# Two 256-column instructions in place of one of 512, for the products of the two gate groups

## The chip, the cores and the metric

The kernel runs on one core of one Trainium2 chip. The metric is device time in microseconds (us) of one execution; smaller is better. The engines that matter here are TensorE (PE in the profile; its weight loads are listed apart as PEld), VectorE (DVE), ScalarE (ACT) and SyncE (SP, which issues the large loads from HBM).

## The reference

One layer of a hybrid encoder, for 256 tokens of width 4096, in float32. Cut to what matters:

```python
xn = rms_norm(x, norm_g)
h = jnp.einsum('bsd,de->bse', xn, w_in)          # w_in: 4096 x 14336
c_val, c_glu, c_gate, q, k, v, a_gate = jnp.split(h, split_pts, axis=-1)   # 2048 each
conv_out = conformer_conv(c_val, c_glu, ...) * jax.nn.silu(c_gate)
attn_out = longnet_mixture(rms_norm(q), rms_norm(k), v, rel_bias) * jax.nn.silu(a_gate)
x = x + jnp.einsum('bse,ed->bsd', concat([conv_out, attn_out]), w_out)     # 4096 x 4096
```

The change concerns the columns `c_gate` of the first product, 2048 of its 14336.

## The kernel before

**The products.** Each float32 operand is split into a high part of reduced width (type `fp32r`) and a low part (the rest, `fp32r` too). A product of two operands is then three matmuls: high by high, low by high, and high by low. The activations are the stationary operand, `xh` and `xl` (for the last product `mh` and `ml`), 128 rows of the contraction by 128 tokens; the weights stream past as the moving operand, `wh` and `wl`, 512 columns an instruction.

**Groups and steps.** The columns of both weight matrices are cut into 18 groups of 1024 columns, in this order: four groups `conv`, four pairs of `agv` and `qk` (attention gate and value, then query and key), two groups `gate`, and four groups `out`. Each group runs over 32 steps `k` of 128 contraction rows. Each step has two halves `e` of 512 columns, and each half has two blocks `s` of 128 tokens; a pair of half and block has an accumulator `acc` of 128x512 float32 in PSUM, a whole PSUM bank. So a step issues 2 halves x 2 blocks x 3 = 12 large matmuls, and the program has 18 x 32 x 12 = 6912 of them, 768 in the two gate groups.

**The order.** It is written by hand: `products(n, e, part)` issues part 0 (lines 668 and 669, with `wh`) or part 1 (line 671, with `wl`) of step n and half e. The loop at the end of the kernel issues half 0 of step n, half 1 of step n-1, and between them `split_w(n + 3)`, in which ScalarE makes `wh` (line 223) and VectorE makes `wl` (line 224) of a later step, and SyncE starts the load of a pair of steps behind it (line 202). `pump()` then adds units of background work: the convolution, norms, transposes, and the attention heads, whose two small float32 products stand on lines 521 (`psc`, scores) and 560 (`po`, values). After the last step of a half `evacuate` reads its two accumulators; for the gate groups this is a Silu on ScalarE (line 626).

Each matmul in the trace has a weight load (LDWEIGHTS, in the row of PEld) of its own, with the same line number.

Of the kernel before, what the change touches and what calls it, by code (L numbers as in the profile page):

```python
# [21 lines left out]
KT = D // P  # L22
# [18 lines left out]


def _bias_index():
    """[33, 512]: one-hot relative-position bucket of delta = column - 255, and in the
    last row the log of how many dilation patterns hold that delta."""
    out = np.zeros((RB + 1, NDEL), np.float32)
    half, exact, dmax = RB // 2, RB // 4, 1024
    for m in range(NDEL):
        d = m - (S - 1)
        n = abs(d)  # L50
        if n < exact:
            b = n
        else:
            b = exact + int(
                np.float32(np.log(np.float32(n) / np.float32(exact)))
                / np.float32(math.log(dmax / exact))
                * np.float32(half - exact)
            )
            b = min(b, half - 1)
        b += half if d > 0 else 0  # L60
        out[b, m] = 1.0
        c = int(n <= 64) + int(n % 4 == 0 and n <= 256) + int(n % 16 == 0 and n <= 1024)
        out[RB, m] = math.log(c) if c else NEG
    return out


class Lane:
    """Background work: generators that yield the weight of a unit on VectorE and ScalarE."""

    def __init__(self, width):  # L70
        self.gens = deque()
# [3 lines left out]
        self.gens.append(gen)  # L75

    def step(self, left):
        """One unit of each of the first generators, while both engines have room left."""
        spent = 0
        for gen in list(self.gens)[: self.width]:  # L80
            if min(left) <= 0:
                break
            try:
                cost = next(gen) or 0
            except StopIteration:
                self.gens.remove(gen)
                continue
            cost = cost if isinstance(cost, tuple) else (cost, 0)
            for i in range(2):
                left[i] -= cost[i]  # L90
            spent += sum(cost)
        return spent
# [3 lines left out]
def layer_kernel(  # L96
# [16 lines left out]
    nc = tc.nc  # L113
# [7 lines left out]
    def t4(name):  # L121
        return sb.tile([P, 4, 256], F32, tag="c4", bufs=15, name=name)
# [7 lines left out]
    def side(name):  # L130
        return ps.tile([P, 512], F32, tag="side", bufs=4, name=name)
# [8 lines left out]
        nc.tensor.transpose(dst, src, ident[:n, :n])  # L140

    def rsqrt(src, shape, mul, eps, name):
        """1 / sqrt(src * mul + eps), one Newton step after the table's square root."""
        n = int(np.prod(shape[1:]))
        tag = "rs_small" if n <= 32 else "rs_big"
        v = sb.tile(shape, F32, tag=tag, bufs=6, name=name + "v")
        r = sb.tile(shape, F32, tag=tag, bufs=6, name=name + "r")
        t = sb.tile(shape, F32, tag=tag, bufs=6, name=name + "t")
        cost = 60 + n
        nc.vector.tensor_scalar(v, src, mul, eps, op0=ALU.mult, op1=ALU.add)  # L150
        yield cost
        nc.scalar.activation(r, v, AF.Sqrt)
        yield
        nc.vector.reciprocal(r, r)
        nc.vector.tensor_mul(t, r, r)
        yield 3 * cost
        nc.vector.tensor_mul(t, t, v)
        nc.vector.tensor_scalar(t, t, -0.5, 1.5, op0=ALU.mult, op1=ALU.add)
        nc.vector.tensor_mul(r, r, t)
        yield 3 * cost  # L160
        return r
# [13 lines left out]
    groups = []  # L175
# [159 lines left out]
    conv_ready = {}  # L335

    def backwards(ap):
        """The last axis read from its end."""
        *lead, (step, n) = ap.ap
        return bass.AP(  # L340
            tensor=ap.tensor, offset=ap.offset + (n - 1) * step, ap=[*lead, [-step, n]]
        )

    def turn(tile_, name, flip=False):
        """[128 tokens, 2, 512 columns] to [128 columns, 4, 256 tokens], in its place: VectorE
        turns the blocks of 32, ScalarE puts them where they belong. With flip, the tokens of
        each half come in reversed order."""
        tmp = t4(name)
        src = tile_.rearrange("p a b -> p (a b)")
        flat = tmp.rearrange("p a b -> p (a b)")  # L350
        for s in range(2):
            nc.vector.transpose(flat[:, 512 * s : 512 * s + 512], src[:, 512 * s : 512 * s + 512])  # L352
            yield 620
        blocks = flat.rearrange("p (s t b x) -> p s t b x", s=2, t=4, b=4)
        dst = src.rearrange("p (t s a x) -> p s t a x", t=4, s=2, a=4)
        for b in range(4):
            for a in range(4):
                v = blocks[32 * a : 32 * a + 32, :, :, b, :]
                to = 3 - a if flip else a
                nc.scalar.copy(  # L360
                    dst[32 * b : 32 * b + 32, :, :, to, :], backwards(v) if flip else v
                )
                if a % 2 == 1:
                    yield 0, 620
# [34 lines left out]
        return bass.AP(tensor=ap.tensor, offset=ap.offset, ap=[ap.ap[0], [0, 4], [1, S]])  # L399

    def channel_mean(srcs, name):
        """Mean over all channels of four [128, 4, 256] tiles, on every partition, in PSUM."""
        tot = sb.tile([P, S], F32, tag="rs_big", bufs=6, name=name + "tot")
        for i, make in enumerate(srcs):
            v = make()
            if i:
                part = sb.tile([P, S], F32, tag="rs_big", bufs=6, name=f"{name}p{i}")
            else:
                part = tot
            nc.vector.reduce_sum(part, v.rearrange("p t s -> p s t"), axis=AX.X)  # L410
            yield 1135
            if i:
                nc.vector.tensor_add(tot, tot, part)
                yield 335
        yield
        yield
        pm = side(name + "pm")
        nc.tensor.matmul(pm[:, :S], ones, tot, start=True, stop=True)
        yield
        return pm  # L420
# [84 lines left out]
    def head_gen(hg, hh):  # L505
# [43 lines left out]
        for b in range(4):  # L549
            for a in range(4):  # L550
                nc.scalar.copy(  # L551
                    dst[32 * b : 32 * b + 32, :, :, 3 - a, :],
                    backwards(blocks[32 * a : 32 * a + 32, :, :, b, :]),
                )
            yield 0, 800
# [33 lines left out]
    left = [0, 0]  # L589

    def pump():
        """Background work for one step of the products: what the engines have room for."""
        for i, quota in enumerate((DVE_STEP, ACT_STEP)):
            left[i] = min(left[i] + quota, quota)
        mix_lane.step(left)
        fg.step(left)
        for _ in range(8):
            if not conv_lane.step(left):
                break
# [47 lines left out]
    accs = {}  # L647

    def products(n, e, part):
        """Products of step n into half e; part 0: with the weights' high parts, 1: with the low."""  # L650
        g, k = divmod(n, KT)
        if k == 0 and part == 0:
            accs[(g, e)] = [
                ps.tile([P, 512], F32, tag="acc", bufs=4, name=f"acc{g}_{e}_{s}") for s in range(2)
            ]
        if g < n_in:
            h, l = xh[k], xl[k]
        else:
            while k not in mh:
                pump()  # L660
            h, l = mh[k], ml[k]
        at = 512 if groups[g][3 + e] > groups[g][4 - e] else 0
        w = w_split[n][part][:, at : at + 512]
        for s in range(2):
            a = accs[(g, e)][s]
            hs, ls = h[:, P * s : P * s + P], l[:, P * s : P * s + P]
            if part == 0:
                nc.tensor.matmul(a, hs, w, start=k == 0, stop=False)  # L668
                nc.tensor.matmul(a, ls, w, start=False, stop=False)  # L669
            else:  # L670
                nc.tensor.matmul(a, hs, w, start=False, stop=k == KT - 1)  # L671
        if part == 1:
            if k == KT - 1:
                evacuate(g, e, accs.pop((g, e)))
            if e == 1:
                del w_split[n]

    load_x(0, 0, P)
    first = load_pair(0, pieces=2)
# [25 lines left out]
    for n in range(NG * KT):  # L705
        g, k = divmod(n, KT)
# [4 lines left out]
        if groups[g][0] == "out" and k in (8, 12):  # L711
            e = (k - 8) // 4
            c = groups[g][3 + e]
            t = t4(f"xr{g}_{e}").rearrange("p a b -> p (a b)").rearrange("p (s c) -> p s c", s=2)
            nc.sync.dma_start(t, xs[:, :, c : c + 512])
            xr_tiles[(g, e)] = t
        products(n, 0, 0)
        if n == 0:
            split_w(1)
# [26 lines left out]
        elif n == 29:  # L746
            list(rstd_steps)
        pump()


_BIAS_INDEX = _bias_index()
_INS = [
    "x", "norm_g", "w_in", "q_norm_g", "k_norm_g", "rel_bias", "conv_w", "conv_b",
# [30 lines left out]
```

## Time and profile before

| | |
|---|---|
| time, median of 2 runs | 1621.97 us (1621.79 to 1622.15) |
| span of the profiled execution, first to last instruction | 1620.2 us |
| PE busy (matmuls, ends modelled) | 1614.1 us, 100% of the span, 7146 instructions |
| PEld busy (weight loads, beside PE) | 1333.3 us, 82%, 7146 |
| DVE busy | 1074.4 us, 66%, 1440 |
| ACT busy | 926.8 us, 57%, 1415 |
| HBM traffic over the span | 196 GB/s |

The 7146 matmuls are the 6912 large ones and 234 small ones. The span stands 1.8 us below the median of the timed runs; that is what lies around the instructions. A matmul's recorded duration overlaps the next one's, so the spacing of their starts, or the chain of waits, tells what one costs; the duration does not.

### The profile page before, as it was taken

The page shows a single profiled execution, that of the slowest core. Times are in us where ns is not written, and L with a number is a line of the kernel's source. Part 1 is how long each engine was busy: PE and PEld are TensorE (multiplying, and loading weights), DVE is VectorE, ACT ScalarE, POOL GpSimd, SP SyncE. Part 2 cuts the span into 40 slices and gives each one's busy share as a digit, 9 for nine tenths or more (in the row PEclk, how much of TensorE's full clock was granted, in tenths as well). Part 3 has the DMA queues.
Part 4 walks back from the last instruction along what each step waited for, and adds up shares of the span by engine and source line. Part 5 has one row for each costly group of instructions (what it writes and reads, how often), then busy time and mean ns, then how long its engine had stood idle before and what let it go on. Part 6 is the DMA issues. An engine that isn't in the chain of part 4 may idle for free.

```text
span 1620.2 us, 19251 instructions
## 1 busy us (share of the span) xinstructions
PE 1614.1 (100%) x7146; PEld 1333.3 (82%) x7146; DVE 1074.4 (66%) x1440; ACT 926.8 (57%) x1415; POOL 2.7 (0%) x10
## 2 busy tenths in 40 slices
PE   9999999999999999999999999999999999999998
PEld 7788888888888888888888888888888888888887
DVE  5567888888888888768765555656466565454543
ACT  6564454545363556774778756774667973333332
POOL 0000000000000000000000000000000000000000
PEclk9999999999999999999999999999999999999999
DMA  8566565656656565656655666556555567666663
GB/s 311 192 188 202 184 204 184 199 191 193 196 189 201 186 203 194 192 160 204 191 187 188 187 202 192 191 166 200 195 197 179 195 214 225 217 218 223 213 228 104
DMA packets 140767, 319.39 MB, mean 197 GB/s; under 512 B 8639, under 2 KB 12049, under 8 KB 140672
## 3 DMA queue, kind: packets, MB, share of 16 engines
q1 hardware_dynamic: 140624, 318.13, 60.5%
q8 instruction: 56, 0.92, 0.2%
q14 instruction: 39, 0.32, 0.1%
q10 hardware_dynamic: 48, 0.02, 0.0%
HBM read 313.89 MB, written 4.23 MB: 196 GB/s over the span
## 4 chain that ended last, share of the span: by engine, by line
PE 99%; ACT 1%; issue 0%; DVE 0%; DVEq 0%
PE acc L668 32%; PE acc L669 32%; PE acc L671 32%; PE psc L521 1%; PE po L560 1%; PE xT L140 0%; ACT wh L223 0%; ACT cT L446 0%; PE spin L695 0%; ACT qk L360 0%; PE pw L140 0%; DVE wl L224 0%; PE pb L327 0%; DVE qk L501 0%; DVE xr L609 0%
## 5 line engine op out<-in xcount | busy, mean ns | idle before, releaser
L224 DVE TENSOR_TENSOR wl<-raw,wh 128x1024 fp32r<-128x1024 f32 x576 | 704.8, 1224 | 509.2 <-ACT wh L223 508.8
L223 ACT CAST wh<-raw 128x1024 fp32r<-128x1024 f32 x576 | 605.8, 1052 | 618.1 <-PE acc L669 412.6
L668 PE MATMUL acc<-wh,xh 128*128 128x512 f32 x1792 | 704.0, 393 | 0.0
L669 PE MATMUL acc<-wh,xl 128*128 128x512 f32 x1792 | 698.0, 390 | 0.0
L671 PE MATMUL acc<-wl,xh 128*128 128x512 f32 x1792 | 490.2, 391 | 0.0
L668 PEld LDWEIGHTS acc<-wh,xh 128*128 128x128 f32 x1792 | 336.5, 188 | 71.3 <-ACT xh L253 0.9
L669 PEld LDWEIGHTS acc<-wh,xl 128*128 128x128 f32 x1792 | 336.5, 188 | 70.2
L671 PEld LDWEIGHTS acc<-wl,xh 128*128 128x128 f32 x1792 | 334.3, 188 | 68.7 <-DVE wl L224 0.4
L392 DVE SCALAR_TENSOR_TENSOR cT<-conv,wT,cT 128x241 f32<-128x241 f32 (+14 forms) x480 | 201.6, 470 | 0.0
L668 PE MATMUL acc<-wh,mh 128*128 128x512 f32 x512 | 199.2, 389 | 0.0
L669 PE MATMUL acc<-wh,ml 128*128 128x512 f32 x512 | 199.2, 389 | 0.0
L671 PE MATMUL acc<-wl,mh 128*128 128x512 f32 x512 | 138.1, 389 | 0.0
L669 PEld LDWEIGHTS acc<-wh,ml 128*128 128x128 f32 x512 | 96.1, 188 | 20.0
L671 PEld LDWEIGHTS acc<-wl,mh 128*128 128x128 f32 x512 | 96.1, 188 | 19.9
L668 PEld LDWEIGHTS acc<-wh,mh 128*128 128x128 f32 x512 | 96.1, 188 | 19.9
L551 ACT COPY pr<-turn_p 32x128 f32<-32x128 f32 x256 | 75.9, 297 | 5.5 <-DVE turn_p L545 2.1
L253 ACT ACTIVATE xh<-xT,g_cols 128x256 fp32r<-128x256 f32 x32 | 15.2, 474 | 34.0 <-PE xT L140 33.9
L360 ACT COPY qk<-turn_q 32x256 f32<-32x256 f32 x64 | 25.9, 404 | 1.2
L360 ACT COPY qk<-turn_k 32x256 f32<-32x256 f32 x64 | 25.8, 404 | 1.2 <-DVE turn_k L352 0.2
L360 ACT COPY conv<-turn_a 32x256 f32<-32x256 f32 x64 | 25.8, 404 | 1.0
L360 ACT COPY agv<-turn_ag 32x256 f32<-32x256 f32 x64 | 25.8, 404 | 1.0
L360 ACT COPY gate<-turn_g 32x256 f32<-32x256 f32 x64 | 25.8, 404 | 1.0
(138 smaller groups left out, 428.0 us busy)
## 6 DMA issues: line engine op xcount, KB each, us to landing
raw<-in_w_in_dram SPq DMA_DIRECT2D x384, 512.0 KB, 4.9
raw<-in_w_out_dram SPq DMA_DIRECT2D x64, 1024.0 KB, 5.4
raw<-in_w_in_dram SPq DMA_DIRECT2D x32, 1024.0 KB, 5.0
xr<-in_x_dram SPq DMA_DIRECT2D x8, 512.0 KB, 6.0
out_dram<-xr SPq DMA_DIRECT2D x16, 256.0 KB, 4.7
x<-in_x_dram SPq DMA_DIRECT2D x6, 512.0 KB, 8.6
T<-bias_dram SPq DMA_DIRECT2D x16, 192.0 KB, 5.0
x<-in_x_dram SPq DMA_DIRECT2D x3, 128.0 KB, 4.2
```

The source lines that it names most:

```text
L223: nc.scalar.copy(wh, src)
L224: nc.vector.tensor_sub(wl, src, wh.bitcast(F32))
L253: nc.scalar.activation(h, pt[:, :S], AF.Copy, scale=g_cols[:, k : k + 1])
L360: nc.scalar.copy(dst[32 * b : 32 * b + 32, :, :, to, :], backwards(v) if flip else v)
L392: nc.vector.scalar_tensor_tensor(c[:, t, lo:hi], a[:, t, lo + sh : hi + sh], wT[:, ch, k : k + 1], c[:, t, lo:hi], op0=ALU.mult, op1=ALU.add,)
L521: nc.tensor.matmul(psc[:, it, :], qt[hg][:, hh, P * it : P * it + P], kt[hg][:, hh, :], start=True, stop=True,)
L551: nc.scalar.copy(dst[32 * b : 32 * b + 32, :, :, 3 - a, :], backwards(blocks[32 * a : 32 * a + 32, :, :, b, :]),)
L560: nc.tensor.matmul(po[:, :S], vt[hg][:, jt, hs], pT[:, jt, :], start=jt == 0, stop=jt == 1)
L668: nc.tensor.matmul(a, hs, w, start=k == 0, stop=False)
L669: nc.tensor.matmul(a, ls, w, start=False, stop=False)
L671: nc.tensor.matmul(a, hs, w, start=False, stop=k == KT - 1)
```

## The change

In the gate groups, each matmul over 512 columns becomes two, over columns 0 to 255 and 256 to 511 of the same accumulator, with the same stationary operand. In part 0 both pieces with the high part of the activations come first, then both with the low part. The start flag, which makes a matmul overwrite its bank instead of adding, stands on the first piece of the first step alone. All other groups keep one span of 512 columns. The comment strings of some functions are removed as well.

```diff
         for s in range(2):
             a = accs[(g, e)][s]
             hs, ls = h[:, P * s : P * s + P], l[:, P * s : P * s + P]
+            spans = [(0, 256), (256, 512)] if groups[g][0] == "gate" else [(0, 512)]
+            for lo, hi in spans:
+                o, v = a[:, lo:hi], w[:, lo:hi]
+                first = k == 0 and lo == 0
+                if part == 0:
+                    nc.tensor.matmul(o, hs, v, start=first, stop=False, skip_group_check=True)
+                else:
+                    nc.tensor.matmul(
+                        o, hs, v, start=False, stop=k == KT - 1, skip_group_check=True
+                    )
             if part == 0:
-                nc.tensor.matmul(a, hs, w, start=k == 0, stop=False)
-                nc.tensor.matmul(a, ls, w, start=False, stop=False)
-            else:
-                nc.tensor.matmul(a, hs, w, start=False, stop=k == KT - 1)
+                for lo, hi in spans:
+                    o, v = a[:, lo:hi], w[:, lo:hi]
+                    nc.tensor.matmul(o, ls, v, start=False, stop=False, skip_group_check=True)
```

The lines move: 668 becomes 672, 669 becomes 680, and 671 becomes 674.

PE, at the border between the last `qk` group (accumulators `acc_1_0`, `acc_1_1`, the end of its half 1) and the first gate group (`acc_0_0`, `acc_0_1`, its first step). Before:

```order
L671 MATMUL acc_1_0_7929<-wl_8567,xh_943 128x512
L671 MATMUL acc_1_1_7930<-wl_8567,xh_943 128x512
L668 MATMUL acc_0_0_8651<-wh_8589,xh_115 128x512
L669 MATMUL acc_0_0_8651<-wh_8589,xl_116 128x512
L668 MATMUL acc_0_1_8652<-wh_8589,xh_115 128x512
L669 MATMUL acc_0_1_8652<-wh_8589,xl_116 128x512
```

PE, the same place with the change (x2 stands for two instructions in a row that read alike):

```order
L674 MATMUL acc_1_0_7929<-wl_8567,xh_943 128x512
L674 MATMUL acc_1_1_7930<-wl_8567,xh_943 128x512
L672 MATMUL acc_0_0_8651<-wh_8589,xh_115 128x256 x2
L680 MATMUL acc_0_0_8651<-wh_8589,xl_116 128x256 x2
L672 MATMUL acc_0_1_8652<-wh_8589,xh_115 128x256 x2
L680 MATMUL acc_0_1_8652<-wh_8589,xl_116 128x256 x2
```

Nothing changes places; from the first gate row on, each row holds two instructions of half the width.

PE, in the middle of the second gate group, where a step ends and a head's score products (`psc`) follow. Before:

```order
L671 MATMUL acc_1_0_9278<-wl_9456,xh_373 128x512
L671 MATMUL acc_1_1_9279<-wl_9456,xh_373 128x512
L671 MATMUL acc_0_0_9258<-wl_9474,xh_416 128x512
L671 MATMUL acc_0_1_9259<-wl_9474,xh_416 128x512
L521 MATMUL psc_9567<-qk_1_8643,qk_0_8624 128x256 x2
```

PE, there with the change:

```order
L674 MATMUL acc_1_0_9672<-wl_9940,xh_373 128x256 x2
L674 MATMUL acc_1_1_9673<-wl_9940,xh_373 128x256 x2
L674 MATMUL acc_0_0_9642<-wl_9970,xh_416 128x256 x2
L674 MATMUL acc_0_1_9643<-wl_9970,xh_416 128x256 x2
L521 MATMUL psc_10101<-qk_1_8643,qk_0_8624 128x256 x2
```

The small products stay where they stood among the steps. On all other engines the same instructions stand in the same order.

## The prediction

> **What bounds the kernel now.** I read the page's busy times and its chain of waits first, then who waits for whom on PE, then the stage of the two gate groups.
>
> ```profile
> span 1620.2 us, 19251 instructions
> PE 1614.1 (100%) x7146; PEld 1333.3 (82%) x7146; DVE 1074.4 (66%) x1440; ACT 926.8 (57%) x1415; POOL 2.7 (0%) x10
> PE 99%; ACT 1%; issue 0%; DVE 0%; DVEq 0%
> ```
>
> A busy PE alone proves little, since its ends are modelled. But the chain that ended last runs through PE for 99% of the span. The view of waits says the same from the other side; these are all its rows for PE:
>
> ```profile
> PE spin L695 <- DVE ones L136: 1.1, 1, 1.1
> PE psc L521 <- DVE qk L501: 0.4, 1, 0.4
> ```
>
> Neither lies in the gate groups' products. In that stage (1086 to 1267 us of the span) the columns are PE, PEld, DVE, ACT and POOL busy, then the granted clock, DMA share and GB/s:
>
> ```profile
> 1086.00:1267.00 181.00, 181.00 (x800) 149.86 (x799) 105.19 (x129) 122.73 (x218) 0.00 (x0) 1.00 0.57 189
> ```
>
> PE is covered for all 181 us at a granted clock of 1.00, while DVE has 76 us left and ACT 58. The 800 matmuls are the 768 large ones and 32 small ones of the heads. So PE's own pace sets the time, and a nanosecond on one large matmul here is a nanosecond times 768.
>
> **The pace of a 512-column matmul.** The chain of waits shows one and a half steps inside the gate stage (start, length, instruction):
>
> ```profile
> 1151.84 0.91 PE acc L671 x4
> 1152.74 0.23 PE acc L668
> ...
> 1154.33 0.23 PE acc L669
> 1154.56 0.91 PE acc L671 x4
> 1155.46 0.23 PE acc L668
> ```
>
> From 1152.74 to 1155.46 are 12 matmuls in 2.72 us, 226.7 ns each; 768 of them make 174.1 us of the stage. The next question is what part of the 226.7 ns depends on the number of columns, because only the rest is paid twice after the split. No large matmul in this trace has other than 512 columns, so I work the parts out from the small float32 matmuls, which have 128 columns (`xT`, line 140) and 256 (`psc`):
>
> ```profile
> 14.64 0.22 PE xT L140 x2
> 1006.80 1.73 PE psc L521 x8
> ```
>
> That is 110 ns for 128 columns and 216 ns for 256: 106 ns for 128 more columns, or 0.83 ns a column, and a fixed rest of about 4 ns. A float32 column is dearer than an fp32r column, since 512 of the latter take 226.7 ns and not 512 x 0.83 = 425. I take it as exactly twice as dear, an estimate that puts an fp32r column at 0.415 ns. Then 512 columns stream in 212.5 ns, and **14.2 ns of each large matmul are fixed**. The choice of the factor two is the weakest link: it is the whole number nearest to 425/226.7 = 1.87, and a fixed part below zero can't be.
>
> **The weight load.** Each piece brings its own load of the same 128x128 stationary operand. Their cost alone shows where PE had been idle and two loads follow each other without a running matmul (row of PEld, the last number is the idle time before):
>
> ```profile
> 7.98 0.19 PEld L671 LDWEIGHTS acc<-wl,xh 128*128 128x128 f32 x1 [0.38 <-DVE wl L224]
> 7.98 0.30 PEld L671 LDWEIGHTS acc<-wl,xh 128*128 128x128 f32 x2 [0.38 <-DVE wl L224]
> ```
>
> One load lasts 0.19 us and two last 0.30, so the second starts 0.11 us after the first: loads follow each other every 110 ns, though one is on record for 190. At 512 columns this hides entirely: 110 + 212 would be 322 ns if it didn't, and the spacing is 226.7. At 256 columns a piece streams for 106 ns, about as long as a load. In the run of steps the load starts with the matmul before it (the first row is the matmul, the second the load for the next one):
>
> ```profile
> 1200.70 0.39 PE L668 MATMUL acc<-wh,xh 128*128 128x512 f32 x1
> 1200.71 0.19 PEld L669 LDWEIGHTS acc<-wh,xl 128*128 128x128 f32 x1
> ```
>
> So the pace of the pieces is the later of the two: about 110 ns for loads, and 106 + 14 = 120.4 ns for matmuls. By these rows the load just fits.
>
> **The change part by part.**
>
> 1. Split of 768 matmuls into 1536: 2 x 120.4 - 226.7 = 14.1 ns for each, on the path, 768 x 14.1 = **+10.8 us**. Bounds: from below, a piece could be as cheap as half a 256-column float32 matmul, 108 ns, which gives 2 x 108 - 226.7 = -10.7 ns and -8.2 us; from above, a piece could last as long as that whole matmul, 216 ns, which gives 205 ns and +157.7 us, and is also what a load and a stream in series would cost (110 + 106). Between ends so far apart I take the value from the 512-column row, since it is of the same type and the same stage.
> 2. 768 more weight loads: 0, hidden beside the matmul in front. If that cover is gone, see the third rival.
> 3. Order of the pieces (both high pieces, then both low ones) and the start flag: 0. The four L671 in a row above write two different accumulators and go at 0.91/4 = 0.2275 us, and the L668 and L669 that write the same one in succession go at 0.23, so which bank comes next shows no price.
> 4. DVE, ACT, SP: the same work in the same order. They only gain time, 11 us over 181; the Silu evacuations are in the same places. Nothing waits for PE that PE waits for later: its waits above are 0.4 us past the start-up, and the first `out` steps run at the same pace.
>
> Sum: 1620.2 + 10.8 = 1631.0 us of span, and with the 1.8 us around it that the median has, **1632.8 us**, up 0.7%. A measurement of this kernel tells about 2%, some 32 us, from no change, so this counts as no change.
>
> **A rule on the fixed part.** The Trainium skill, "TensorE: Matmul & The Clock Gate", § Back-to-back issue gap, puts the warm gap at N/2.4 + 2.5 ns, so 215.8 ns for 512 columns and 109.2 for 256. By that rule the split would add only 2.5 ns for each, an estimate of +1.9 us. The trace disagrees with it for these matmuls: 226.7 ns, at a granted clock of 1.00. Where it does hold is the float32 row's small rest of some 4 ns.
>
> **A rule against the change.** The same page, § The mechanism, says that a weight load overlaps running matmuls only when it goes to another row group; every load here fills all 128 rows, so load and stream would be in series and the split would add a whole load for each matmul. The trace of this case disagrees at 512 columns, where load and stream in series would be 322 ns against 226.7.
>
> **The rivals.**
>
> *The extra part goes with the columns, or is paid once for one set of weights.* If the 14 ns are a slower stream (226.7/512 = 0.443 ns a column), a piece takes 113.3 ns and the sum is 0: 1622 us; with float32's 4 ns for each extra instruction it is +3 us, 1625. For it: only one width of fp32r is in the trace, so the split of 226.7 rests on float32 rows. Against it: the float32 rows show a stream that fits 0.415 with a factor two. Chance 0.18.
>
> *The load becomes the pace, mildly.* The load needs 110 ns, and if the 14 ns is an exchange of weights that can only start when the load has ended, a piece takes 124 to 127 ns: up to 2 x 127 - 226.7 = 27 ns, 768 x 27 = +21 us, 1643. For it: 110 is within 10 ns of the 120 that must cover it. Against it: `psc` changes weights with each of its matmuls and has almost no fixed part. Chance 0.16.
>
> *The load becomes the pace, in full; this one ends slower by over 2%.* If the next matmul may only begin at the recorded end of its load, and the next load only with that matmul, a piece takes the whole 188 ns of a load and the few ns to the next start, some 191 ns: 2 x 191 - 226.7 = 155 ns, +119 us, 1741. Load and stream in series give +158 us, 1780. It decides from 134 ns a piece, where 768 x (2 x 134.5 - 226.7) passes 32 us. For it, the recorded length of a load in the stage:
>
> ```profile
> L668 PEld LDWEIGHTS acc<-wh,xh 128*128 128x128 f32 x1792 | 336.5, 188 | 71.3 <-ACT xh L253 0.9 <-ACT wh L223 0.4
> ```
>
> Against it: the two loads 110 ns apart, which couldn't be if the array were taken for 188. Chance 0.11.
>
> *Cheaper pieces.* If the fixed 14 ns were something that a shorter matmul escapes, the lower bound of step 1 holds: 1614 us. No row speaks for it. Chance 0.03. Faster by over 2% would need pieces of 92 ns, below the stream itself; I leave 0.01 for that.
>
> That the change doesn't do what it says is excluded by the order: all 768 rows of the gate groups hold two instructions of 256 columns, each with its load.
>
> **How the numbers follow.** The forecast, 1628 to 1637 us, has 0.51. Range: from 1620, just below the first rival, to 1645, just past the second; it leaves out the full load pace, the cheaper pieces and the rest, some 15 in 100. Faster by over 2%: 0.01; slower: 0.12 (the third rival and a little for contention that no row shows); within 2%: 0.87.
>
> **What would show it.** The profile after should have 7914 matmuls and 7914 loads; the chain in the gate stage at 0.24 us for a pair of pieces and 2.89 us a step instead of 2.72; the stage at about 192 us instead of 181, all other stages as before; PEld's busy time near 100% there, since 188 ns loads would follow each other every 120; and no new wait on PE. A pair at 0.227 speaks for the first rival, one at 0.25 for the second, above 0.27 for the third. The prediction is wrong if loads don't hide behind 256 columns, or if a stall appears at the changes between small float32 matmuls and pieces.

## The result, and the profile after

The changed kernel takes 1631.72 us (2 runs, 1631.66 to 1631.77) against 1621.97 us before: a ratio of 1.0061, with a 95% interval of 1.0045 to 1.0077. It is 9.75 us slower, where 10.8 were forecast. The interval leaves out 1, so the kernel is slower, but by less than the 2% below which a change is counted as none.

The page of the changed kernel, in the rows that answer to those of before (span, busy times, the chain by engine):

```profile
span 1629.9 us, 20787 instructions
PE 1623.6 (100%) x7914; PEld 1373.7 (84%) x7914; DVE 1074.7 (66%) x1440; ACT 926.8 (57%) x1415; POOL 2.7 (0%) x10
PE 98%; ACT 1%; DMA 0%; issue 0%; DVE 0%; SPq 0%; DVEq 0%
```

The span is 9.7 us longer, like the time. There are 768 more matmuls, each with a load, and the busy times of DVE and ACT are the same to 0.3 us. PE is the chain as before. The view of waits has its two old rows for PE and one more, of the start:

```profile
PE xT L140 <- DMA x<-in_x_dram: 0.2, 1, 0.2
```

The gate stage now ends at 1277 us instead of 1267 (columns PE, PEld, DVE, ACT, POOL busy, clock, DMA share, GB/s):

```profile
1086.00:1277.00 191.00, 191.00 (x1569) 190.14 (x1568) 105.32 (x130) 123.70 (x220) 0.00 (x0) 1.00 0.55 180
```

The granted clock is 1.00 as before, so no slower clock explains the time. DVE and ACT do in 191 us what they did in 181. PEld is busy for 190.1 of 191 us: loads on record at 189 ns follow each other so closely that they overlap. That looks like an engine at its limit and isn't one, as the chain shows:

```profile
1152.67 0.96 PE acc L674 x8
1153.63 0.24 PE acc L672 x2
1153.87 0.24 PE acc L680 x2
...
1155.31 0.24 PE acc L680 x2
1155.55 0.48 PE acc L674 x4
```

From 1152.67 to 1155.55 is one step, 24 pieces (the shorter matmuls that take the place of one) in 2.88 us, **120.0 ns a piece**. The step took 2.72 us before, and the two gate groups have 64 steps: 64 x 0.16 us = 10.2 us.

The two widths together give the fixed part without any other matmul: 256 columns more take 226.7 - 120.0 = 106.7 ns, so, if the price is a straight line, a column takes 0.4167 ns, and 226.7 - 512 x 0.4167 = 13.3 ns are left for each matmul. The theory to be tested: a large matmul costs 0.4167 ns a column and 13.3 ns for itself, and its load is hidden. The main rival: 120 ns is the pace of the loads, and only by chance near 106.7 + 13.3.

### The profile page after: what moved, and what is told of

Read it like the earlier page. It is cut to its first block, busy times and chain, and to the rows that moved or that the text cites. A ratio compares the mean times of both kernels' runs of the same rounds, so it can differ in the third digit from the quotient of the medians.

```text
span 1629.9 us, 20787 instructions
## 1 busy us (share of the span) xinstructions
PE 1623.6 (100%) x7914; PEld 1373.7 (84%) x7914; DVE 1074.7 (66%) x1440; ACT 926.8 (57%) x1415; POOL 2.7 (0%) x10
## 4 chain that ended last, share of the span: by engine, by line
PE 98%; ACT 1%; DMA 0%; issue 0%; DVE 0%; SPq 0%; DVEq 0%
PE acc L672 32%; PE acc L680 32%; PE acc L674 32%; PE psc L521 1%; PE po L560 1%; PE xT L140 0%; DMA x<-in_x_dram 0%; ACT wh L223 0%; ACT cT L446 0%; ACT qk L360 0%; PE pw L140 0%; DVE wl L224 0%; PE pb L327 0%; SPq L211 0%; SPq L244 0%
## 5 line engine op out<-in xcount | busy, mean ns | idle before, releaser
L672 PE MATMUL acc<-wh,xh 128*128 128x512 f32 (+1 forms) x2048 | 707.7, 366 | 0.0
L680 PE MATMUL acc<-wh,xl 128*128 128x512 f32 (+1 forms) x2048 | 701.5, 363 | 0.0
L674 PE MATMUL acc<-wl,xh 128*128 128x512 f32 (+1 forms) x2048 | 493.5, 364 | 0.0
L672 PEld LDWEIGHTS acc<-wh,xh 128*128 128x128 f32 x2048 | 368.8, 189 | 61.6 <-ACT xh L253 0.9
L680 PEld LDWEIGHTS acc<-wh,xl 128*128 128x128 f32 x2048 | 368.4, 189 | 60.2
L674 PEld LDWEIGHTS acc<-wl,xh 128*128 128x128 f32 x2048 | 352.6, 189 | 58.3 <-DVE wl L224 0.2
```

Source lines behind the costliest of these rows:

```text
L672: nc.tensor.matmul(o, hs, v, start=first, stop=False, skip_group_check=True)
L674: nc.tensor.matmul(o, hs, v, start=False, stop=k == KT - 1, skip_group_check=True)
L680: nc.tensor.matmul(o, ls, v, start=False, stop=False, skip_group_check=True)
```

## Experiments

All times are to be held against the 1622 us of before. Each run's chain is read in the gate stage, as above. Diffs are against the changed kernel where nothing else is said.

### Shorter pieces: where the load becomes the pace

Run `q128`, four pieces of 128 columns:

```diff
-            spans = [(0, 256), (256, 512)] if groups[g][0] == "gate" else [(0, 512)]
+            spans = [(128 * q, 128 * q + 128) for q in range(4)] if groups[g][0] == "gate" else [(0, 512)]
```

> Each large matmul of the gate groups becomes four of 128 columns. My theory: a piece costs its columns at 0.417 ns plus 13.3 ns, unless its weight load takes longer; loads follow each other every 110 ns, so here, for the first time, the load sets the pace: pieces 110 to 113 ns apart, 440 to 452 ns for each old matmul instead of 226.7, +164 to +173 us, 1786 to 1795 us. Rival, the load was the pace already at 256 columns and its pace is 120 ns: 480 ns, +195 us, 1817 us. Second rival, the load never sets the pace: 4 x 66.7 = 267 ns, +31 us, 1653 us.

Measured: 1790.03 us, ratio 1.1034 (1.101 to 1.1058). The chain (x4 are the pieces of one old matmul):

```profile
1150.66 1.79 PE acc L674 x16
1152.44 0.45 PE acc L672 x4
1152.89 0.45 PE acc L680 x4
```

1.79/16 is 112 ns a piece. It is below 120, so the load's pace is not 120, and the rival falls: in the change the load was hidden, with 8 ns to spare (`u288` below shows the same pace for pieces of 224 columns). It is far above 53.3 + 13.3 = 66.7, so here the load does set the pace.

Run `u384`, with `spans = [(0, 384), (384, 512)]`: as many matmuls as in the change, and a slower kernel.

> The same number of pieces as in the change, but 384 and 128 columns instead of 256 and 256. My theory: 173.3 ns for the long piece and the load's 110 to 113 ns for the short one (its stream alone would be 66.7), 283 to 286 ns for each old matmul, +43 to +46 us, 1665 to 1668 us. Rival, a load pace of 120 ns: 293 ns, +51 us, 1673 us. Second rival, only the number of matmuls counts and the load never sets the pace: 240 ns as in the change, 1632 us.

Measured: 1668.6 us, ratio 1.0285 (1.0263 to 1.0308).

```profile
1150.07 1.15 PE acc L674 x8
1151.22 0.29 PE acc L672 x2
...
1153.51 1.15 PE acc L674 x8
```

From 1151.22 to 1153.51 are 8 pairs, 286 ns each: 173.3 ns for 384 columns by the theory, and 113 for the short piece, the pace of the load. Only the sum is measured. The starts in the trace divide it otherwise, 228 ns from a long piece to the short one and 58 from there to the next long one; that fits the theory if the long piece is on record as started while its load, begun only with the short piece, still runs.

Run `u288`, with `spans = [(0, 288), (288, 512)]`:

> As the change, but 288 and 224 columns. My theory: 288 columns 133.3 ns; 224 columns would stream in 106.7 ns, just under the load's 110 to 113, so the pair takes 243 to 246 ns, +13 to +15 us, 1635 to 1637 us. Rival, a load pace of 120 ns: 253 ns, +20 us, 1642 us. Second rival, the load never sets the pace: 240 ns, 1632 us.

Measured: 1636.01 us, ratio 1.0085 (1.0065 to 1.0106); 245 ns a pair:

```profile
1152.58 0.24 PE acc L672 x2
...
1154.54 0.49 PE acc L674 x4
```

(8 pairs from 1152.58 to 1154.54.) The excess over 240 is again what a 224-column piece lacks of the load's 112. The pairs of `u384` and `u288` hold the same load and differ by 96 columns and 41 ns, 0.43 ns a column, close to the 0.4167 of the straight line. So 256 and 256 is the cheapest of the three ways to split in two, and here a piece has to last 112 ns to hide its load.

### The price times a larger number

Run `all256`, with `spans = [(0, 256), (256, 512)]` in all groups:

> All 6912 large matmuls are split into halves of 256 columns, not only the 768 of the gate groups. My theory, 13.3 ns for each extra matmul and nothing else: 6144 more than in the change, +81.9 us on 1631.7, 1713.6 us. Rival, part of the price is made good elsewhere or the other engines take part: a figure off that by more than 5 us, or pieces that are not 120 ns apart in the convolution stage, where VectorE is busiest.

Measured: 1710.95 us, ratio 1.0546 (1.0524 to 1.0569), 2.7 us less than expected. The pieces stand 120 ns apart here too; a step in the gate stage:

```profile
1151.49 0.24 PE acc L672 x2
...
1153.41 0.96 PE acc L674 x8
1154.37 0.24 PE acc L672 x2
```

Ten of the 18 groups hold no small matmuls and no start or end; in each of them the trace before has 384 matmuls in 87.04 us, and this one 768 in 92.16, first start to the next group's first start, which is 226.67 and 120.0 ns a matmul. The missing microseconds lie elsewhere: the span grew by 88.5 us, not by 6912 x 13.33 = 92.2, and of the 3.7 us between, 1.5 are in the first group, where PE also waits for its inputs, and the rest nearly all in the groups with heads. There, before, the step behind a head's small matmuls was slower than others; here the burst of small ones itself was longer too:

```profile
1188.10 1.84 PE psc L521 x8
1189.94 0.23 PE acc L668
...
1192.70 0.23 PE acc L668
```

From 1189.94 to 1192.70 it took 2.76 us, against 2.72. In the changed kernel the same step has no such excess:

```profile
1193.95 1.73 PE psc L521 x8
1195.67 0.24 PE acc L672 x2
...
1198.55 0.24 PE acc L672 x2
```

That is 2.88 us, as for any other, and the burst takes 1.73 us instead of 1.84. The gate stage has six such bursts; before, they and the steps behind them ran over by 0.02 to 0.16 us each, and with the change by nothing. In the change this takes 0.4 us off the 10.2: the stage grew from 181.4 to 191.2 us, first large matmul to the first one behind it.

### Does it matter which matmul is next?

Run `alt`, in which a half's low product follows its high one at once:

```diff
             for lo, hi in spans:
...
                 if part == 0:
                     nc.tensor.matmul(o, hs, v, start=first, stop=False, skip_group_check=True)
+                    nc.tensor.matmul(o, ls, v, start=False, stop=False, skip_group_check=True)
...
-            if part == 0:
-                for lo, hi in spans:
-                    o, v = a[:, lo:hi], w[:, lo:hi]
-                    nc.tensor.matmul(o, ls, v, start=False, stop=False, skip_group_check=True)
```

> As the change, but in part 0 each half of the columns gets its high and then its low product, so that consecutive pieces have different stationary operands (in the change two pieces in a row share one). My theory, the price is one of each matmul whatever its neighbour: pieces 120 ns apart, 1631.7 us. Rival, a second load of the same operand is cheaper in part: part 0 dearer here, by up to the difference between 120 and 134 ns for 1024 pieces, +14 us, 1646 us. Second rival, two writes in a row to the same half of a bank cost time: also slower than 1631.7.

Measured: 1631.84 us, ratio 1.0059 (1.0041 to 1.0077), the same as the change, with pieces 120 ns apart; a step:

```profile
1151.02 0.12 PE acc L672
...
1153.90 0.12 PE acc L672
```

From 1151.02 to 1153.90 it takes 2.88 us as in the change. Neither a repeated stationary operand nor two writes to the same half in a row has a price.

Run `part1`, with the split only where `part == 1`:

> Only the products with the weights' low parts in the gate groups are split, a third of the change: 256 more matmuls. My theory: 256 x 13.3 = +3.4 us, 1625.4 us, pieces 120 ns apart and whole ones 226.7. Rival, mixing the two widths costs or saves something at the borders: another figure than a third of the change's 10.2 ns per thousand.

Measured: 1626.35 us, ratio 1.0027 (1.0017 to 1.0038): +4.4 us instead of 3.4. The interval, 2.8 to 6.2 us, holds both, but the trace shows the rival, a price for mixing the widths:

```profile
1150.38 0.95 PE acc L674 x8
1151.33 0.23 PE acc L672
...
1152.95 0.23 PE acc L680
1153.17 0.95 PE acc L674 x8
```

The eight whole matmuls between take 1.84 us, 230 ns each instead of 226.7, while the pieces take 0.95/8 = 119. So the 512-column matmuls among shorter ones, like those behind the small matmuls above, take a few ns more each. It isn't a price of every switch: the pieces of 256 columns behind the small matmuls show none. What does that inside PE stays open.

### Whose are the 13.3 ns?

Run `m64`, against the kernel before:

```diff
...
-                nc.tensor.matmul(a, hs, w, start=False, stop=k == KT - 1)
+                m = 64 if groups[g][0] == "gate" and k < KT - 1 else P
+                nc.tensor.matmul(
+                    a[:m], hs[:, :m], w, start=False, stop=k == KT - 1, skip_group_check=True
+                )
```

> The kernel before, with 512 columns; in the gate groups the products with the weights' low parts use only the first 64 of the 128 stationary columns (64 tokens of each block), but for the last step: these products are left out for the other tokens. The load there has half the columns. My theory, the fixed part belongs to the matmul: 226.7 ns as before, 1622 us. Rival, it is the part of the load that can't be hidden, a fixed share of the loaded columns: 220 ns for these 248 matmuls, -1.7 us in all, to be read from the spacing.

Measured: 1623.92 us, ratio 1.001 (1.0 to 1.0021). The loads got shorter, the matmuls didn't (loads of the stage by group, then the chain; line 672 is the narrow product):

```profile
L672 PEld LDWEIGHTS acc<-wl,xh 128*64 128x64 f32 (+1 forms) x244 | 33.0, 135 | 19.6
```

```profile
1152.71 0.92 PE acc L672 x4
```

A load on record at 135 ns instead of 188 gives 230 ns a matmul. The run is 2 us slower than before, because the whole matmuls of its mixed sequence take some 229 ns too, so a few ns of mixing lie over the reading. But the narrow ones are not faster than the whole ones, where the rival put them 6.7 ns below: the 13.3 ns are not a share of the load's columns.

Runs `bf512` (against the kernel before), `bf256` and `bfq128` (against the change and `q128`) read both operands of the gate groups as bfloat16, in 512, 256 and 128 columns:

```diff
+    def bf(ap):
+        (p, n), (step, cols) = ap.ap
+        v = ap.bitcast(mybir.dt.bfloat16)
+        (p2, n2), _ = v.ap
+        return bass.AP(tensor=v.tensor, offset=v.offset + 1, ap=[[p2, n2], [2, cols]])
...
+            if groups[g][0] == "gate":
+                hs, ls, w_ = (bf(t) for t in (hs, ls, w))
```

In the matmuls `w_` then stands in place of `w`.

> The kernel before, with 512 columns; in the gate groups both operands are read as bfloat16, the upper halves of the same words, so the lower bits of the operands are left out there. It asks whether the fixed part belongs to the 4-byte type. My theory doesn't say; if it belongs to fp32r, matmuls 214 to 217 ns apart, 768 x -11 = -8 us, 1614 us; if to every matmul with a load of its own, 226.7 ns and 1622 us. Rival, reading every second 2-byte element makes the stream slower: over 227 ns.

> As the change (pieces of 256 columns), with both operands of the gate groups read as bfloat16, the upper halves of the same words, so the operands' lower bits are left out there. At 512 columns such matmuls stood 225 ns apart. My theory, a fixed part that each matmul pays whatever its type and the length of its load: 106.7 + 11.7 = 118 ns a piece, stage 181 us and some 1631 us in all. Rival, the fixed part is there a slower stream (225/512 ns a column): 112.5 ns a piece, 1621 us.

> Pieces of 128 columns as in the run q128, but read as bfloat16 (the operands' lower bits are left out in the gate groups). There the load of 110 to 112 ns set the pace. Bfloat16 loads are on record at 96 ns instead of 188. My theory, once the load is short the fixed part shows again: 53.3 + 11.7 = 65 ns a piece, 260 ns for each old matmul, +27 us on the 1621.1 us at 512 columns, 1648 us. Rival, the load is still the pace, or another floor under a matmul with its load: over 70 ns a piece, over 1664 us.

Measured: 1621.08, 1621.42 and 1623.79 us; ratios 0.9993 (0.9983 to 1.0004), 0.9998 (0.9987 to 1.0009) and 1.0012 (1.0001 to 1.0023). The products with the weights' low parts, a row from each run's chain in that order:

```profile
1152.13 0.90 PE acc L681 x4
```

```profile
1151.37 0.91 PE acc L683 x8
```

```profile
1152.46 0.92 PE acc L683 x16
```

They give 225, 113 and 57 ns. Splitting a bfloat16 matmul in two or four costs next to nothing, so my theory that each matmul of any type pays the fixed part is wrong; and with a load on record at 96 ns even 57 ns a piece hides it. But the 225 ns at 512 columns still hid something, since 225 - 213.3 could have been taken for a fixed part.

Runs `bfc512` and `bfc256` let the moving operand be neighbouring words (step 1 instead of 2 for `w`), in 512 and 256 columns:

> As the run bf512 (bfloat16 in the gate groups, 512 columns), but the moving operand is 512 neighbouring 2-byte words instead of every second one, so the weights of the gate groups are replaced by other numbers there. It asks why bfloat16 at 512 columns stood 225 ns apart while its split cost nothing. If every second word makes the stream slower, the matmuls stand 214 to 217 ns apart here, some -8 us, 1614 us. If 0.436 ns a column is what these matmuls need in this kernel, 225 ns and 1621 us.

> As bfc512, in pieces of 256 columns. If the fixed part of a bfloat16 matmul is the 2 ns that the split to 256 and 128 columns of every second word showed, 108 to 109 ns a piece, 1615 us; if it is the 13 ns of fp32r, 120 ns a piece, 1632 us.

Measured: 1613.95 us, ratio 0.995 (0.9931 to 0.997), and 1615.5 us, ratio 0.9963 (0.9947 to 0.9978). The same row in each:

```profile
1153.71 0.86 PE acc L681 x4
```

```profile
1151.93 0.87 PE acc L683 x8
```

That is 215 and 109 ns. So every second word cost about 10 ns in 512 columns (the numbers that stream past are others too, and no run separates the two), and bfloat16 has a fixed part of 2 to 3 ns. **The 13.3 ns belong to fp32r matmuls.** Whether the matmul itself or the exchange of a 4-byte stationary operand takes them was not settled: no fp32r matmul ran without a load of its own. The float32 `psc` speak against the exchange: each brings a 4-byte load on record at some 189 ns, and at 216 ns for 256 columns, of 0.83 ns each (twice 0.4167), some 3 ns are left. That is an argument, not a test.

## Why the prediction was right

- *PE's pace sets the time*: right. The change of the span is the change of PE's step.
- *Fixed part, 14.2 ns, from float32 rows and a factor of two*: right in kind, 0.9 ns too large. The factor of two, called the weakest link, holds: 0.4167 ns against 0.83. That it came out so close is in part luck. The row of 0.22 us for two `xT` is rounded to 10 ns, so one of them takes 107.5 to 112.5, and this alone lets the fixed part be anything from 9 to 19 ns. Besides, 110 ns for an `xT` is also the pace of the loads (110 by the row of two loads, 112 in `q128`), so the row can't tell a stream of 128 columns from a load; and `xT` is a transpose while `psc` is a product, so the two need not lie on one line.
- *Step 1, +10.8 us*: 10.2 by the measured pace, and 9.8 in the stage, as the excess around the small matmuls went away. That term of 0.4 us was missing from the sum.
- *Step 2, hidden loads*: right, and closer than it read: 112 ns of load under 120 ns of matmul. The row of two loads 110 ns apart told this, not their 188 ns. It did not show loads without a running matmul, as the prediction read it, since the first one's matmul was on record from 7.99 us and the second load came at 8.09; that the pace holds in a run of steps too came out of `q128`, at 112 ns.

```profile
7.99 0.50 PE L671 MATMUL acc<-wl,xh 128*128 128x512 f32 x1
```

- *Step 3, order, banks and start flag, 0*: right, by `alt` for the order and the banks. The start flag had no run of its own; the step of 24 pieces at 120.0 ns leaves it nothing.
- *Step 4, the other engines*: right, by the busy times above.
- *What would show it*: 2.89 us a step was named, 2.88 measured; 192 us for the stage, 191; PEld near 100% there, 99.5%. The small matmuls brought no stall. One wait on PE is new, 0.2 us at the start, outside the gate stage.
- *The rival of a slower stream* is false for fp32r and true for bfloat16 read in every second word. *The rival of the load as the pace, mildly*, is false at 256 columns. At 224 and 128 the load does set the pace, but at 112 ns and not at the 124 to 127 of an exchange that starts after the load. *The rival of the full 188 ns* is false at any width here: 112 ns a piece came out of `q128`.
- *The rule of the Trainium skill on the gap* ("TensorE: Matmul & The Clock Gate", § Back-to-back issue gap, which gives N/2.4 + 2.5 ns for the warm gap of a single matmul and not for a stream of loads and matmuls) makes it 215.8 and 109.2 ns. The streams with neighbouring bfloat16 words agree all the same, at 215 and 109; fp32r, at 226.7 and 120.0, does not.
- *The rule on overlap* (the Trainium skill, same page, § The mechanism), by which the prediction put load and stream in series, is contradicted at 256 columns too: 110 + 107 ns against 120. The section also lets a load into a background weight buffer go ahead of running matmuls, which the prediction left out; these runs show the overlap, not where the load goes.

## What to carry to other kernels

Where one engine is the whole chain, find its price as a line through two sizes of the same kind of instruction, a part for each column and a part for each instruction; only the second is paid again when an instruction is split. Then look for the hidden partner of the short instruction, here the load, and take its pace from the spacing of two starts, not from its duration. What is hidden has a width at which it no longer is: here 256 columns cost 0.6%, and 128 columns 10.3%.

## What was not expected of the hardware

An fp32r matmul of 512 columns takes 226.7 ns and a bfloat16 one 215, at the same clock; the difference is per instruction, since at 256 columns it is 120.0 against 109. Reading every second 2-byte word as the moving operand costs about 4% (225 against 215 ns). The 512-column fp32r matmuls of a mixed sequence run a few ns slower than alone: 230 against 226.7 in `part1`. In fp32r the loads follow each other every 112 ns (`q128`) though one is on record for 188.
